# A sixth modulation block's sums moved behind two row products, its broadcasts moved one group on, four residual loads moved back, and another first PSUM bank

## The chip, the cores and the metric

The kernel runs on one core of a Trainium2 chip. Its time is the device time of one execution in microseconds (us); lower is better. A core has five engines that work beside each other and wait for each other through semaphores: TensorE (PE, matmuls), VectorE (DVE), ScalarE (ACT), GpSimd (POOL) and SyncE (SP, which here issues most of the transfers). Each engine takes its instructions in the order in which the program gives them.

## What is computed

One layer of a residual block over 1024 positions of width 1024, in float32. Six rows of 1024 (shift, scale and gate for each of two halves) come from the conditioning vector c through `w_ada`; the sixth, `gate2`, is the block that this change is about.

```python
c_act = jax.nn.silu(c)
mod = (c_act @ w_ada[l] + b_ada[l])[:, None, :]
shift1, scale1, gate1, shift2, scale2, gate2 = jnp.split(mod, 6, axis=-1)
h = rms_norm(x, norm1_w[l]) * (1.0 + scale1) + shift1
x = x + gate1 * hybrid_mixer(h, w_in[l], ...)      # projections, gated DeltaNet, short conv, @ w_out
h = rms_norm(x, norm2_w[l]) * (1.0 + scale2) + shift2
x = x + gate2 * swiglu(h, w_gate[l], w_up[l], w_down[l])
...
return rms_norm(x, norm_f_w)
```

## The kernel before

Positions are cut into eight tiles of 128; tiles 0 to 3 are the first half, 4 to 7 the second. A matmul has 512 columns; a float32 product is made of three matmuls of high and low parts, so each operand is split by a cast (high part) and a subtraction (low part).

Up to about 499 us of the span the order of work is planned by a small scheduler in Python (class `Sim`, line 296): tasks are coroutines, each operation is a request with a modelled cost, and the scheduler picks, engine by engine, the one that can start first, with priorities (`PR`, line 43) where several can. Its pick is written into the program as a fixed order on each engine. A task waits with `sim.wait(...)` for marks in the set `done`; a buffer or a PSUM bank is asked for and freed. Every operation of this part is recorded at line 440; what comes after it is written in program order and is recorded at lines 91 and 92. The profile therefore tells groups apart by the names of their tiles.

The pieces that matter here:

- `fill` (line 937) ends with the output projection of the first half: eight groups of 24 matmuls into tiles named `o`, first the right column half of tiles 0 to 3, then the left one. They take turns in three PSUM banks (0 to 2). `ev_o` adds each to the residual tile `x2[t]`, which the profile calls `x`. The weights for the left half (`us0`, in slots called `h`) are loaded from `w_out`, scaled and split by `w_unit` while the groups run.
- `load_y` brings the second half's products of the short convolution back from DRAM (`raw<-y_scr`) and splits them into `WQ`.
- `mod_rows` (line 1049) makes a row out of the scale column of the second norm: twice, DVE multiplies an identity by the column (`raw<-ident,s2c`), the result is split, two matmuls with a matrix of ones spread it to all partitions (tile `row`), and a copy stores it in `su` (called `u`).
- `gate5` and `ada_rows` (lines 1012 and 990) make `gate2`: for each column half eight weight tiles of 128 x 512 are loaded (`Tt<-in_w_ada_dram` and `raw<-in_w_ada_dram`), DVE sums them with `c_act` as scalars into `A` and `aacc`, the sum is split, two matmuls with ones spread it (tile `ada`), and DVE adds it to `gate`, which holds the bias. `gate` is used by `prep_gate` (line 1759), after 580 us.
- `norm0` stores tiles 0 to 3 of `x` to DRAM (`x_scr<-x`) and scales them for the second norm. It waits for `row` and for both halves of `gate5`.
- `coordinator` (line 1413) loads the residual tiles `x2` at its end, one SP transfer of 512 KB each, in the order of t.
- Behind the scheduler, `w_out_tile` does the output projection of tiles 4 to 7, `first_half` transposes the scaled tiles. They take PSUM banks in turn from `allb` (line 1472).

SP gives its transfers out in order, so one that waits for a buffer holds those behind it.

Of the kernel before, what the change touches and what calls it, by code (L numbers as in the profile page):

```python
# [10 lines left out]
F32R = mybir.dt.float32r  # L11
BF16 = mybir.dt.bfloat16
AF = mybir.ActivationFunctionType
ALU = mybir.AluOpType
# [3 lines left out]
P = 128  # L18
# [35 lines left out]
def kernel(  # L54
# [53 lines left out]
    def nm(s):  # L108
        n_id[0] += 1
        return f"{s}_{n_id[0]}"  # L110
# [185 lines left out]
    class Sim:  # L296
# [18 lines left out]
        def free(self, t):  # L315
            res, i = self.owner.pop(t.tensor.name)
            res.slots.append((max([a[4] for a in self.acc.get(t.tensor.name, [])] + [0.0]), i))
            res.slots.sort()
# [238 lines left out]
    def bank(res, name):  # L557
        return res.tile(psp, [P, HT], F32, name)

    def gt(tag, shape=(P, 4, P), dtype=F32):  # L560
        return GP[tag].tile(gp, list(shape), dtype, tag)

    def raw(shape=(P, HT), dtype=F32):
        return raws.tile(wst, list(shape), dtype, "raw")
# [10 lines left out]
    def esplit(src, hi, lo):  # L575
        ecopy(hi, src)
        DVE.tensor_tensor(lo, src, hi.bitcast(F32), ALU.subtract)
# [412 lines left out]
    def ada_rows(b, ch, ac=None, get=None):  # L990
        if ac is None:
            ac = wst.tile([P, HT], F32, name=nm("aacc"), tag="aacc", bufs=1)
        get = get or raw
        c0 = b * D + ch * HT
        for kk in range(KB):
            r = get()
            dma(r, wada[kk * P:(kk + 1) * P, c0:c0 + HT])
            if kk == 0:
                DVE.tensor_scalar(ac, r, c_act[:, 0:1], None, ALU.mult)
            else:  # L1000
                DVE.scalar_tensor_tensor(ac, r, c_act[:, kk:kk + 1], ac, ALU.mult, ALU.add)
            free(r)
        hl = [raw(dtype=F32R) for _ in range(2)]
        esplit(ac, hl[0], hl[1])
        ps = bank(chb, "ada")
        mm(ps, ones_r, hl[0], True, False)
        mm(ps, ones_r, hl[1], False, True)
        for t in hl:
            free(t)
        return ps  # L1010

    def gate5(ch):
        sim.wait(lambda: len(us0) == KB and len(us1) == KB and ("gdn", 1) in done)
        if 5 not in gates:
            g = gates[5] = wst.tile([P, D], F32, name=nm("gate"), tag="gate", bufs=1)
            dma(g, b_ada[0, 5 * D:6 * D].partition_broadcast(P))
        gc = gates[5][:, ch * HT:(ch + 1) * HT]
        ac = gt("A", (P, HT)) if ch else None
        ps = ada_rows(5, ch, ac, (lambda: gt("Tt", (P, HT))) if ch else None)
        done.add(("g5", ch))  # L1020
        DVE.tensor_tensor(gc, gc, ps, ALU.add)
        free(ps)
        if ch:
            free(ac)

# [387 lines left out]
    def coordinator():  # L1413
        nonlocal gp, x2p, b1p
        sim.wait(lambda: "ada0" in done)
        wa_ctx.__exit__(None, None, None)
        b1 = tc.tile_pool(name="b1", bufs=1, side="right", reuse_waits="tile")
        b1p = b1.__enter__()
        for hd in (0, 1):
            qkT[hd, 0] = qks.tile(b1p, [P, 2, HT], F32, "qkT")  # L1420
        done.add("b1")
        sim.wait(lambda: "h1" in done)
        x_ctx.__exit__(None, None, None)
        s_ctx.__exit__(None, None, None)
        pools["g"] = tc.tile_pool(name="gp", bufs=2, side="left", reuse_waits="tile")
        gp = pools["g"].__enter__()
        for i in range(4):
            xbd.append(gp.tile([P, 4, P], F32, name=f"xbd{i}", tag=f"xbd{i}", bufs=1))
        for t in xbd:
            POOL.memset(t, 0.0)  # L1430
        done.add("gp")
        sim.wait(lambda: "filled" in done and live[0] == 0 and all(("vt", 1, h) in done for h in heads) and
                 all(("sc", i, hf) in done and ("z", i, hf) in done for i in range(4) for hf in range(2)))
        b1.__exit__(None, None, None)
        pools["x2"] = tc.tile_pool(name="x2p", bufs=1, side="right", reuse_waits="tile")
        x2p = pools["x2"].__enter__()
        for t in range(NT):
            x2.append(x2p.tile([P, D], F32, name=f"x2_{t}", tag=f"x2_{t}"))
        for t in range(NT):
            sim.wait(lambda: len(us1) + len(us0) > min(5 + t, 12) and (t < 4 or ("chain", 1) in done))  # L1440
            dma(x2[t], xs[t * P:(t + 1) * P, :])
            done.add(("x2", t))

# [25 lines left out]
    mover[0], chain[0] = None, seq  # L1469
    g_ctx, x2_ctx = pools["g"], pools["x2"]  # L1470

    allb = Banks(list(range(8)))

    def gt(tag, shape=(P, 4, P), bufs=2):
        return gp.tile(list(shape), F32, name=nm(tag), tag=tag + "0", bufs=1)
# [3 lines left out]
    def pmm(o, l, r, s_, e_, more=False):  # L1479
        pe("pe", PE.matmul(o, l, r, start=s_, stop=e_, skip_group_check=more))  # L1480
# [31 lines left out]
    def keep_x2(t, chs):  # L1512
        for ch in chs:
            cs = slice(ch * HT, (ch + 1) * HT)
            ACT.dma_start(out=x2_scr[t][:, cs], in_=x2[t][:, cs])
# [41 lines left out]
        DVE.tensor_tensor(x2[t][:, cs], x2[t][:, cs], ps, ALU.add)  # L1557


    e_raw, e_u = {}, {}  # L1560

    def early_load(n):
# [13 lines left out]

    w_out_tile(4, 1)
    keep_x2(4, (1,))
    w_out_tile(4, 0)
    norm_tile(4)  # L1580
    first_half(range(4))
# [556 lines left out]
```

## Time and profile before

| | us |
|---|---|
| median of 3 runs | 1192.98 |
| lowest and highest of them | 1191.99, 1194.83 |
| the profiled execution's own time | 1194.26 |
| its span, first to last instruction | 1192.4 |
| mean granted clock of TensorE | 0.996 |

A row of the profile gives the engine, the line, the operation and `out<-in` by the names of tiles, the shape and a count; in the timeline a row starts with its start and length, and ends in brackets with the engine's idle time ahead of it and who ended that. Matmuls overlap, so their pitch is read from the length of many, not from a single one.

### The profile page before, as it was taken

Reading aid. Unit: us, or ns where it says so; the run is one execution under the profiler, and the core shown is the slowest. Engines: PE = TensorE matmul, PEld = TensorE weight load, DVE = VectorE, ACT = ScalarE, POOL = GpSimd, SP = SyncE. Lnnn points to the kernel's source line nnn. Section 1 sums busy time; section 2 is a strip of 40 time slices with the busy share of each in tenths; the row PEclk is TensorE's granted clock in tenths of the full one; section 3 lists DMA queues with packets and bytes.
Section 4 is the critical chain, followed back from the end, with each engine's and each line's share of the span. In section 5 each row is a group of like instructions: output and inputs, shape, how many; then the busy total and the mean of one; then the engine's idle time right before and its main releaser. Section 6 shows DMA issues by size and latency. Waiting matters only on the chain.

```text
span 1192.4 us, 16796 instructions
## 1 busy us (share of the span) xinstructions
PE 1173.7 (98%) x5723; PEld 984.7 (83%) x5723; DVE 928.9 (78%) x1738; ACT 529.3 (44%) x1118; POOL 57.2 (5%) x95
## 2 busy tenths in 40 slices
PE   8999999999999998999999999999999999999997
PEld 7888878988888987788888888888888888888886
DVE  6998989799977798757786767777767787688676
ACT  3488732359632544224543333333333365434343
POOL 2010000001000001100000000000000000000003
PEclk9999999999999999999999999999999999999999
DMA  9933455544425447423344564465544679869413
GB/s 289 299 81 111 133 171 161 160 115 136 111 47 130 136 133 271 174 77 98 124 157 161 191 225 157 142 205 185 198 165 140 211 275 397 311 199 346 144 42 141
DMA packets 175775, 207.08 MB, mean 174 GB/s; under 512 B 21829, under 2 KB 107978, under 8 KB 175690
## 3 DMA queue, kind: packets, MB, share of 16 engines
q1 hardware_dynamic: 170312, 202.85, 53.0%
q10 hardware_dynamic: 5378, 3.16, 0.9%
q8 instruction: 45, 0.74, 0.3%
q14 instruction: 40, 0.33, 0.1%
HBM read 150.91 MB, written 55.05 MB: 173 GB/s over the span
## 4 chain that ended last, share of the span: by engine, by line
PE 91%; DMA 3%; DVE 3%; ACT 1%; issue 1%; SPq 0%; DVEq 0%; ACTq 0%
PE acc L91 34%; PE acc L440 24%; PE dn L91 17%; PE o L91 4%; PE o L440 2%; PE A L440 1%; PE K L440 1%; DMA raw<-y_scr 1%; PE ada L440 1%; DMA x<-in_x_dram 1%; DMA raw<-in_w_ada_dram 1%; PE ab L440 1%; PE Q L440 1%; PE w L440 1%; PE u L440 1%; PE O L440 1%
## 5 line engine op out<-in xcount | busy, mean ns | idle before, releaser
L440 PE MATMUL acc<-h,u 128*128 128x512 f32 x1200 | 302.6, 398 | 0.0
L440 PEld LDWEIGHTS acc<-h,u 128*128 128x128 f32 x1200 | 219.0, 188 | 41.2
L91 PE MATMUL acc<-h,hl 128*128 128x512 f32 x600 | 140.0, 390 | 0.0
L91 PEld LDWEIGHTS acc<-h,hl 128*128 128x128 f32 x600 | 112.4, 188 | 23.2
L91 PE MATMUL acc<-h,u 128*128 128x512 f32 x456 | 106.1, 389 | 0.0
L91 PE MATMUL acc<-T,hl 128*128 128x512 f32 x432 | 101.3, 390 | 0.2 <-ACT cc L92 0.2
L91 PEld LDWEIGHTS acc<-h,u 128*128 128x128 f32 x456 | 85.6, 188 | 17.8
L91 PEld LDWEIGHTS acc<-T,hl 128*128 128x128 f32 x432 | 80.9, 188 | 17.3 <-ACT cc L92 0.6
L92 DVE TENSOR_TENSOR xo<-xo,dn 128x512 f32<-128x512 f32 x84 | 57.2, 686 | 44.0 <-PE dn L91 36.2
L91 PE MATMUL dn<-h,h 128*128 128x512 f32 x396 | 90.7, 389 | 0.0
L91 PEld LDWEIGHTS dn<-h,h 128*128 128x128 f32 x396 | 74.3, 188 | 15.4
L92 ACT COPY cc<-acc 128x512 f32<-128x512 f32 x66 | 38.5, 591 | 108.3 <-PE acc L91 108.3
L91 PE MATMUL acc<-T,u 128*128 128x512 f32 x360 | 84.0, 389 | 0.0
L91 PEld LDWEIGHTS acc<-T,u 128*128 128x128 f32 x360 | 67.6, 188 | 14.0
L440 ACT CAST u<-raw 128x512 fp32r<-128x512 f32 x64 | 39.8, 623 | 70.7 <-PE acc L440 64.1
L92 DVE TENSOR_TENSOR cc<-cc,acc 128x512 f32<-128x512 f32 x66 | 43.9, 684 | 29.8 <-PE acc L91 29.8
L440 DVE TENSOR_TENSOR u<-raw,u 128x512 fp32r<-128x512 f32 x82 | 56.2, 686 | 12.8 <-ACT u L440 12.0
L92 DVE TENSOR_TENSOR hl<-R,hl 128x512 fp32r<-128x512 f32 x60 | 39.5, 689 | 33.4 <-ACT hl L92 33.4
L440 DVE SCALAR_TENSOR_TENSOR cv<-pr,cols_b,cv 128x512 f32<-128x512 f32 x72 | 53.1, 747 | 1.2 <-ACT cv L440 0.9
L92 ACT CAST h<-rw 128x512 fp32r<-128x512 f32 x57 | 32.7, 618 | 41.0 <-PE dn L91 34.6
L92 DVE TENSOR_TENSOR u<-R,u 128x512 fp32r<-128x512 f32 x46 | 30.1, 688 | 20.5 <-ACT u L92 20.5
L92 ACT CAST hl<-R 128x512 fp32r<-128x512 f32 x60 | 35.6, 620 | 23.4 <-DVE R L92 10.7
(330 smaller groups left out, 2033.7 us busy)
## 6 DMA issues: line engine op xcount, KB each, us to landing
raw<-in_w_in_dram SPq DMA_DIRECT2D x82, 256.0 KB, 3.2
am_scr<-cc SPq DMA_DIRECT2D x77, 256.0 KB, 4.7
raw<-in_w_ada_dram SPq DMA_DIRECT2D x56, 256.0 KB, 3.3
rw<-am_scr SPq DMA_DIRECT2D x55, 256.0 KB, 5.0
rw<-bm_scr SPq DMA_DIRECT2D x53, 256.0 KB, 5.2
bm_scr<-raw SPq DMA_DIRECT2D x51, 256.0 KB, 5.6
R<-in_w_gate_dram SPq DMA_DIRECT2D x22, 512.0 KB, 4.1
R<-in_w_up_dram SPq DMA_DIRECT2D x22, 512.0 KB, 5.2
```

Source lines behind the costliest of these rows:

```text
L91: return call(*a, **k)
L92: ins = call(*a, **k)
L440: ins = call(*a, **k)
```

## The change

Four things. First, `gate5` starts on the mark `row` instead of the mark of the second half's chain, so its sums are planned after both row products. Second, its spreading matmuls and the adds into `gate` leave the scheduler: the split sums stay in four `Tt` tiles, and a new function `g5_rows` makes the matmuls in program order, behind the first group of `w_out_tile`. Third, the loads of residual tiles 4 to 7 wait for both halves of `gate5` instead of the chain. Fourth, `allb` starts at bank 5 instead of bank 0. The amount of arithmetic and of transfers is the same.

```diff
--- before.py
+++ after.py
@@ -990,6 +990,7 @@
     def ada_rows(b, ch, ac=None, get=None):
         if ac is None:
             ac = wst.tile([P, HT], F32, name=nm("aacc"), tag="aacc", bufs=1)
+        row = get is None
         get = get or raw
         c0 = b * D + ch * HT
         for kk in range(KB):
@@ -1000,8 +1001,10 @@
             else:
                 DVE.scalar_tensor_tensor(ac, r, c_act[:, kk:kk + 1], ac, ALU.mult, ALU.add)
             free(r)
-        hl = [raw(dtype=F32R) for _ in range(2)]
+        hl = [raw(dtype=F32R) if row else gt("Tt", (P, HT), F32R) for _ in range(2)]
         esplit(ac, hl[0], hl[1])
+        if not row:
+            return hl
         ps = bank(chb, "ada")
         mm(ps, ones_r, hl[0], True, False)
         mm(ps, ones_r, hl[1], False, True)
@@ -1009,17 +1012,16 @@
             free(t)
         return ps
 
+    g5 = {}
+
     def gate5(ch):
-        sim.wait(lambda: len(us0) == KB and len(us1) == KB and ("gdn", 1) in done)
+        sim.wait(lambda: len(us0) == KB and len(us1) == KB and "row" in done)
         if 5 not in gates:
             g = gates[5] = wst.tile([P, D], F32, name=nm("gate"), tag="gate", bufs=1)
             dma(g, b_ada[0, 5 * D:6 * D].partition_broadcast(P))
-        gc = gates[5][:, ch * HT:(ch + 1) * HT]
         ac = gt("A", (P, HT)) if ch else None
-        ps = ada_rows(5, ch, ac, (lambda: gt("Tt", (P, HT))) if ch else None)
+        g5[ch] = ada_rows(5, ch, ac, (lambda: gt("Tt", (P, HT))) if ch else raw)
         done.add(("g5", ch))
-        DVE.tensor_tensor(gc, gc, ps, ALU.add)
-        free(ps)
         if ch:
             free(ac)
 
@@ -1437,7 +1439,7 @@
         for t in range(NT):
             x2.append(x2p.tile([P, D], F32, name=f"x2_{t}", tag=f"x2_{t}"))
         for t in range(NT):
-            sim.wait(lambda: len(us1) + len(us0) > min(5 + t, 12) and (t < 4 or ("chain", 1) in done))
+            sim.wait(lambda: len(us1) + len(us0) > min(5 + t, 12) and (t < 4 or ("g5", 0) in done and ("g5", 1) in done))
             dma(x2[t], xs[t * P:(t + 1) * P, :])
             done.add(("x2", t))
 
@@ -1469,7 +1471,7 @@
     mover[0], chain[0] = None, seq
     g_ctx, x2_ctx = pools["g"], pools["x2"]
 
-    allb = Banks(list(range(8)))
+    allb = Banks([5, 6, 7, 3, 4, 0, 1, 2])
 
     def gt(tag, shape=(P, 4, P), bufs=2):
         return gp.tile(list(shape), F32, name=nm(tag), tag=tag + "0", bufs=1)
@@ -1557,6 +1559,14 @@
         DVE.tensor_tensor(x2[t][:, cs], x2[t][:, cs], ps, ALU.add)
 
 
+    def g5_rows():
+        for ch in range(2):
+            ps = allb.get("row")
+            pmm(ps, ones_r, g5[ch][0], True, False)
+            pmm(ps, ones_r, g5[ch][1], False, True)
+            cs = slice(ch * HT, (ch + 1) * HT)
+            DVE.tensor_tensor(gates[5][:, cs], gates[5][:, cs], ps, ALU.add)
+
     e_raw, e_u = {}, {}
 
     def early_load(n):
@@ -1576,6 +1586,7 @@
 
     w_out_tile(4, 1)
     keep_x2(4, (1,))
+    g5_rows()
     w_out_tile(4, 0)
     norm_tile(4)
     first_half(range(4))
```

Since a scheduler decides the order, three places show what moved. The first is DVE at the end of the fifth output group's inputs. Before (`raw_4978`, `raw_5024`: the two diagonals; `raw_4984`, `raw_5028`: their low parts; `h_1_921`: the last weight part of `us0`; `A`, `aacc`: the sums):

```order
L440 SCALAR_TENSOR_TENSOR raw_4828<-raw_4828,cols_a,gate_1301 128x512
L440 TENSOR_TENSOR raw_4984<-raw_4978,raw_4983 128x512
L440 TENSOR_TENSOR x_3_4748<-x_3_4748,o_4951 128x512
L440 TENSOR_TENSOR h_1_921_4994<-raw_4828,h_1_921_4994 128x512
L440 TENSOR_SCALAR A_5010<-Tt_5011,c_act 128x512
L440 TENSOR_TENSOR raw_5024<-ident,s2c 128x512
L440 TENSOR_SCALAR aacc_5013<-raw_5014,c_act 128x512
L440 SCALAR_TENSOR_TENSOR A_5010<-Tt_5021,c_act,A_5010 128x512
L440 TENSOR_TENSOR raw_5028<-raw_5024,raw_5027 128x512
```

And in the changed kernel (`raw_4974`, `raw_5010`: the diagonals):

```order
L440 SCALAR_TENSOR_TENSOR raw_4825<-raw_4825,cols_a,gate_1301 128x512
L440 TENSOR_TENSOR raw_4980<-raw_4974,raw_4979 128x512
L440 TENSOR_TENSOR x_3_4748<-x_3_4748,o_4943 128x512
L440 TENSOR_TENSOR h_1_921_4990<-raw_4825,h_1_921_4990 128x512
L440 TENSOR_TENSOR raw_5010<-ident,s2c 128x512
L440 TENSOR_TENSOR raw_5013<-raw_5010,raw_5012 128x512
L440 TENSOR_SCALAR A_5033<-Tt_5034,c_act 128x512
L440 TENSOR_SCALAR aacc_5036<-raw_5037,c_act 128x512
L440 SCALAR_TENSOR_TENSOR A_5033<-Tt_5041,c_act,A_5033 128x512
```

The second diagonal and its low part stood behind one and three steps of the sums; now all four operations of the row products are ahead of the first step.

The second place is DVE some twenty operations earlier, where the second half's y tiles are split. Before:

```order
L440 TENSOR_TENSOR Tt_4346<-y_4835,Tt_4346 128x512
L440 SCALAR_TENSOR_TENSOR so_4836<-so_4836,nq_3641 128x4
L440 TENSOR_TENSOR h_1_895_4846<-raw_4764,h_1_895_4846 128x512
L440 TENSOR_TENSOR kt_4871<-Tt_4346,at_4870 128x512
L440 TENSOR_TENSOR x_1_4746<-x_1_4746,o_4814 128x512
L440 TENSOR_TENSOR Tt_4347<-y_4860,Tt_4347 128x512
L440 TENSOR_TENSOR u_3345<-u_3345,ro_4838 128x512
```

Now:

```order
L440 TENSOR_TENSOR Tt_4346<-y_4831,Tt_4346 128x512
L440 SCALAR_TENSOR_TENSOR so_4832<-so_4832,nq_3641 128x4
L440 TENSOR_TENSOR h_1_895_4842<-raw_4764,h_1_895_4842 128x512
L440 CAST WQ_4797<-raw_4782 128x512
L440 TENSOR_TENSOR kt_4867<-Tt_4346,at_4866 128x512
L440 TENSOR_TENSOR x_1_4746<-x_1_4746,o_4811 128x512
L440 TENSOR_TENSOR Tt_4347<-y_4856,Tt_4347 128x512
L440 TENSOR_TENSOR u_3345<-u_3345,ro_4834 128x512
```

One cast, `WQ_4797<-raw_4782`, is new on DVE; it was ScalarE's before. Around it the low parts of `WQ` and the gated outputs (`Tt`, `kt`) stand in a slightly other order.

The third place is SP's queue of transfers behind the loads of tiles 0 to 3. Before:

```order
L440 DMA x_2_4747<-in_x_dram 128x1024
L440 DMA x_3_4748<-in_x_dram 128x1024
L440 DMA x_4_4749<-in_x_dram 128x1024
L440 DMA x_5_4750<-in_x_dram 128x1024
L440 DMA raw_4782<-y_scr 128x512
L440 DMA raw_4793<-y_scr 128x512
L440 DMA x_6_4751<-in_x_dram 128x1024
L440 DMA raw_4809<-in_w_out_dram 128x512
L440 DMA x_7_4752<-in_x_dram 128x1024
L440 DMA raw_4828<-in_w_out_dram 128x512
L440 DMA raw_4918<-y_scr 128x512
L440 DMA raw_4937<-y_scr 128x512
```

Now, at the same place:

```order
L440 DMA x_2_4747<-in_x_dram 128x1024
L440 DMA x_3_4748<-in_x_dram 128x1024
L440 DMA raw_4782<-y_scr 128x512
L440 DMA raw_4792<-y_scr 128x512
L440 DMA raw_4807<-in_w_out_dram 128x512
L440 DMA raw_4825<-in_w_out_dram 128x512
L440 DMA raw_4909<-y_scr 128x512
L440 DMA raw_4924<-y_scr 128x512
```

and further on, behind the sixteen loads of `w_ada`:

```order
L440 DMA Tt_5119<-in_w_ada_dram 128x512
L440 DMA raw_5124<-in_w_ada_dram 128x512
L440 DMA x_4_4749<-in_x_dram 128x1024
L440 DMA x_5_4750<-in_x_dram 128x1024
L440 DMA x_6_4751<-in_x_dram 128x1024
L440 DMA x_7_4752<-in_x_dram 128x1024
L440 DMA x_scr<-x_0_4745 128x1024
```

Tiles 4 to 7 have gone from among the y and weight loads to a place between the last load of `w_ada` and the stores of tiles 0 to 3.

## Prediction

> **What bounds the kernel now.** The page's first part comes first: TensorE (PE) is busy for nearly the whole span, so only its idle time, and time at a lower clock, can be won without removing matmuls.
>
> ```profile
> PE 1173.7 (98%) x5723; PEld 984.7 (83%) x5723; DVE 928.9 (78%) x1738; ACT 529.3 (44%) x1118; POOL 57.2 (5%) x95
> ```
>
> Then the view by windows (columns: stretch, its length, busy time and count for each engine, granted clock, DMA share, GB/s), cut at the stages and at 5 us around the place of the change:
>
> ```profile
> 200.00:444.00 244.00, 244.00 (x1416) 212.74 (x1414) 210.07 (x465) 122.73 (x300) 14.01 (x15) 1.00 0.44 123
> 444.00:500.00 56.00, 51.56 (x232) 41.79 (x231) 46.81 (x75) 23.27 (x62) 8.62 (x10) 0.97 0.67 238
> 500.00:580.00 80.00, 79.83 (x407) 66.84 (x406) 53.11 (x79) 30.75 (x59) 4.69 (x11) 1.00 0.34 112
> ...
> 455.00:460.00 5.00, 5.00 (x26) 4.10 (x25) 4.88 (x10) 3.33 (x13) 1.60 (x3) 1.00 1.03 405
> ...
> 475.00:480.00 5.00, 2.49 (x6) 2.01 (x7) 4.08 (x7) 0.62 (x1) 0.00 (x0) 0.70 0.76 270
> 480.00:485.00 5.00, 5.00 (x23) 4.11 (x22) 3.52 (x6) 0.59 (x1) 0.00 (x0) 0.96 0.87 278
> ...
> 495.00:500.00 5.00, 4.22 (x19) 3.20 (x18) 3.24 (x4) 0.93 (x2) 1.76 (x2) 1.00 0.23 92
> ```
>
> PE is never idle from 200 to 444 us and for 0.17 us from 500 to 580 us; between them, from 444 to 500 us, it loses 4.4 us and a part of its clock. This is the stretch where the output projection's last groups, the row products and the sixth modulation block meet, and all that the change touches lies in it. PE's timeline shows the two gaps (in brackets: idle before, and who ended it):
>
> ```profile
> 469.11 0.40 PE L440 MATMUL o<-h,h 128*128 128x512 f32 x1
> ...
> 470.74 3.11 PE L440 MATMUL o<-h,h 128*128 128x512 f32 x13
> 477.51 0.79 PE L440 MATMUL row<-raw,ones 128*128 128x512 f32 x1 [3.66 <-ACT raw L440]
> ...
> 492.25 6.06 PE L440 MATMUL o<-h,h 128*128 128x512 f32 x26
> 499.10 0.50 PE L91 MATMUL o<-L,WQ 128*128 128x512 f32 x1 [0.78 <-DVE x L440]
> 499.43 0.39 PE L91 MATMUL o<-wu,WQ 128*128 128x512 f32 x1
> ```
>
> The chain of work that ended last (start, length, what) says why the first one arises:
>
> ```profile
> 469.94 5.70 DMA Tt<-in_w_ada_dram
> ...
> 475.66 0.49 DVE A L440
> 476.15 0.61 DVE raw L440
> ...
> 476.84 0.63 ACT raw L440
> ...
> 477.51 0.79 PE row L440
> 478.30 1.71 PE o L440 x4
> 480.01 0.43 PE row L440
> 480.44 10.25 PE o L440 x45
> ```
>
> VectorE (DVE) takes its queue in order. The first step of the sums (`A<-Tt`) stood there for its load, and behind it the diagonal (`raw<-ident,s2c`) of the second row product. ScalarE's cast, and with it PE's `row` matmul in the middle of the fifth output group, waited for that.
>
> **The change part by part.** One matmul at full clock takes 10.25 / 45 = 0.2278 us (last row).
>
> *Sums behind the row products.* The DVE order of the changed kernel has both row products ahead of the first sum. Gap: 470.74 + 13 x 0.2278 = 473.70 to 477.51, so 3.81 us. Behind it PE ran slowly: six matmuls from 477.51 to 480.44 took 2.93 us, against 6 x 0.2278 = 1.37; 1.56 us lost. Together 5.37 us, if the second row product isn't late for another reason. The trace shows the granted clock at 0.70 there, and the four matmuls at 478.30 at 0.43 us each. [...]
>
> What is late next? The fifth group starts at 469.11 if nothing before it moves. Its second row product stands after 18 matmuls (469.11 + 4.10 = 473.21) with the high part and after 21 (473.89) with the low part. DVE sets when they are ready:
>
> ```profile
> 454.18 0.43 DVE L440 CAST h<-raw 128x512 fp32r<-128x512 f32 x1
> 455.04 0.69 DVE L440 TENSOR_TENSOR u<-u,ro 128x512 f32<-128x512 f32 x1 [0.44 <-POOL ro L440]
> ...
> 456.32 0.68 DVE L440 TENSOR_TENSOR h<-raw,h 128x512 fp32r<-128x512 f32 x1
> ...
> 461.23 0.69 DVE L440 TENSOR_TENSOR u<-u,ro 128x512 f32<-128x512 f32 x1 [0.29 <-POOL ro L440]
> ...
> 470.64 0.68 DVE L440 TENSOR_TENSOR h<-raw,h 128x512 fp32r<-128x512 f32 x1
> 475.66 0.49 DVE L440 TENSOR_SCALAR A<-Tt,c_act 128x512 f32<-128x512 f32 x1 [4.34 <-DMA Tt<-in_w_ada_dram]
> ```
>
> From 456.32 to 471.32 it has hardly a gap. The changed order brings the same operations up to that last `h<-raw,h`, and one cast more (0.43), which ScalarE did before: 471.75. The diagonal adds 0.61, ScalarE's cast 0.63 with some 0.1 of hand-over, DVE's low part 0.68: 472.36, 473.1, 473.8. PE wants them at 473.21 and 473.89: on time, by a tenth. If the two POOL waits (0.44 and 0.29) close up it is on time by 0.8; if a load holds DVE up, PE waits. I put 0.4 us for a new wait here, between none and the 1.8 of the first rival, nearer to none since every row but the load speaks for it.
>
> *Banks from elsewhere.* The first group written in program order took bank 0, still to be read by DVE after the last scheduled group; now it takes bank 5. The gap 492.25 + 26 x 0.2278 = 498.17 to 499.10 is 0.93, and the first matmul took 0.33 in place of 0.23: 1.03 us. Banks 6, 7 and 3 follow, which the chain stage's transposes and the row products used last.
>
> *Broadcasts among the second half's groups.* Four matmuls and two DVE adds leave the seventh group and come after the first program-order group: 4 x 0.23 us on PE in both kernels, no gain. The adds go to where DVE waits for PE; these rows cover them:
>
> ```profile
> 501.81 1.28 DVE L440 SCALAR_TENSOR_TENSOR x<-x,st,u 128x1024 f32<-128x1024 f32 x1 [2.77 <-DMA x_scr<-x]
> 504.94 0.69 DVE L92 TENSOR_TENSOR x<-x,o 128x512 f32<-128x512 f32 x1 [1.85 <-PE o L91]
> 510.49 0.69 DVE L92 TENSOR_TENSOR x<-x,o 128x512 f32<-128x512 f32 x1 [4.86 <-PE o L91]
> ```
>
> Without that cover they would cost 1.2 us. The new wait, PE on the split sums, is met: ScalarE's view has the second sum's cast, the last but one step of the splits, at
>
> ```profile
> 490.47 0.62 ACT L440 CAST raw<-aacc 128x512 fp32r<-128x512 f32 x1
> ```
>
> and PE comes to them one group after the last scheduled one: 498.17 - 6.4 + 24 x 0.2278 = 497.2.
>
> *Later residual loads.* Tiles 4 to 7 move on SP's queue from among the y and weight loads to behind the 16 weight loads of the sums. SP's timeline (start, length, count):
>
> ```profile
> 450.83 0.94 SPq L440 DMA_DIRECT2D raw<-y_scr  x2
> ...
> 483.40 0.44 SPq L440 DMA_DIRECT2D raw<-in_w_ada_dram  x1
> 484.05 15.34 SPq L440 DMA_DIRECT2D x_scr<-x  x4
> ```
>
> The issues of 440 to 510 us by group (count, size, median us to landing):
>
> ```profile
> x<-in_x_dram SPq DMA_DIRECT2D x8, 512.0 KB, 6.8
> ...
> raw<-in_w_ada_dram SPq DMA_DIRECT2D x8, 256.0 KB, 5.7
> x_scr<-x SPq DMA_DIRECT2D x4, 512.0 KB, 2.6
> ...
> raw<-y_scr SPq DMA_DIRECT2D x4, 256.0 KB, 8.6
> ```
>
> The y loads lose 2.1 MB ahead of them, 5.2 us at 405 GB/s, so they land earlier, not later; nothing on PE waited for them alone, so I count nothing. Tile 4 is wanted when its first group ends, at 497.2. Issued near 484 behind a weight load that lands at 483.4 + 5.7 = 489.1, all four are in by 489.1 + 5.2 = 494.3. Nothing waits.
>
> **Sum.** 5.37 + 1.03 - 0.4 = 6.0 us. Against the profiled execution (1194.26 us, span 1192.4) this gives 1188.3; that execution lies 1.3 us above the median of the runs shown (1192.98), from which the same gain gives **1187.0**. Everything behind 500 us hangs on PE (0.17 us idle up to 580) and shifts with it.
>
> **The rivals.** *First: the gap shrinks but stays.* The DVE cast that is new needs the first y load. Issued a little ahead of the old 450.83, say 450.3, and landing after the old median of 8.6, it comes at 458.9; DVE would reach it at 457.0. Then all of DVE is 1.9 late and PE waits 475.7 - 473.9 = 1.8: gain 6.4 - 1.8 = 4.6, 1188.4. Against it: the 2.1 MB ahead are gone, and without those the load lands near 456. *Second: PE gains nothing.* What PE needs behind the row product, the last weight part (`h<-raw,h`), was done at 471.32 and can't hold it until 477.5. But the first transposes want x tiles 0 to 3 scaled. Before, the last scaling ended at 501.81 + 1.28 = 503.09, while PE came to the transposes 11.4 us after 499.10, at 510.5. Now PE comes at 504.1: if the scaling stayed where it was the margin would be 1.0 us. A scaling 6 us later than before would give all back: 1193. *Third, slower than before.* The scaling of tile 3 also waits until its store has read the tile, and the stores of tiles 0 to 3 now stand behind the four loads. With the loads done at 494.3, four stores of 0.52 MB at 405 GB/s end at 499.5, and about 1 us of landing and 1.28 of scaling give 501.8; margin 2.3 us. For each us beyond it PE waits one, and a wait over 3.7 us would bring the slow clock (1.56) again; so from a delay of 2.3 + 4.9 = 7.2 us on it is slower than before: at 10 us late PE waits 7.7, pays 1.56 more and has won 6.4: 1195.8. For it speaks this row, where loads issued one behind another took up to 10 us to land, against 2.6 for a store alone:
>
> ```profile
> DMA to landing us min/median/max: 6.0/6.8/10.0
> ```
>
> [...] Against the rival: it needs three times the margin that these rows leave.
>
> **How the numbers follow.** Forecast 0.75, about 1187 (1185.0 to 1188.6: a median of few runs moved from 1191.99 to 1194.83); first rival 0.12 (1188 to 1190.5); second 0.07 (1191 to 1194); third 0.06 (1193 to 1197). The range 1185.0 to 1190.6 takes in the forecast and the first rival, and the bounds of the new wait. A measurement of this kernel tells 0.2% (2.4 us) from no change: faster by more than that 0.87 (forecast and first rival), within it 0.08 (the second, and a little of the third), slower 0.05.
>
> **What would show it.** In the changed kernel's windows: 470 to 485 us with PE busy throughout and the clock at 1.00; a `row` matmul with an idle time under 1 us; no idle time ahead of the first L91 matmul; the first L91 transposes some 6 us earlier and without a wait; DVE's first `A<-Tt` still waiting for its load, now with nobody behind it. The prediction is wrong if PE waits over 2 us at `row`, if the transposes wait for `x`, or if a gap appears behind 500 us that wasn't there.

## The result, and the profile after

| | us |
|---|---|
| before, median of 6 runs beside the changed kernel (lowest, highest) | 1193.53 (1191.99, 1195.70) |
| changed, median of 6 runs (lowest, highest) | 1187.32 (1186.06, 1189.51) |
| ratio, 95% interval | 0.9949 (0.9934 to 0.9964) |
| the profiled execution of the changed kernel: its time, its span | 1186.41, 1184.6 |
| mean granted clock of TensorE | 0.998 |

The medians differ by 6.2 us; 6.0 were forecast, and 1187.0 for the time. First, the page's first line of the changed kernel:

```profile
PE 1171.7 (99%) x5723; PEld 984.3 (83%) x5723; DVE 928.4 (78%) x1739; ACT 528.4 (45%) x1117; POOL 55.6 (5%) x95
```

The work is the same, and PE's share has risen from 98 to 99%. The view by windows (columns as before: stretch, length, busy time of PE, PEld, DVE, ACT and POOL, clock, DMA share, GB/s):

```profile
444.00:500.00 56.00, 56.00 (x259) 46.05 (x258) 47.07 (x76) 22.20 (x61) 9.38 (x12) 1.00 0.68 248
...
475.00:480.00 5.00, 5.00 (x24) 4.14 (x23) 5.00 (x8) 0.00 (x0) 0.00 (x0) 1.00 1.04 386
480.00:485.00 5.00, 5.00 (x24) 4.14 (x23) 4.32 (x8) 0.14 (x1) 0.00 (x0) 1.00 1.04 397
485.00:490.00 5.00, 5.00 (x24) 4.14 (x23) 2.48 (x4) 4.24 (x8) 1.56 (x5) 1.00 1.02 410
```

PE is busy for all 56 us from 444 to 500, where it was busy for 51.56, and the clock, 0.70 and 0.96 between 475 and 485 us before, is 1.00. The chain of waits of the changed kernel (start, length, what) is PE alone through the place of the change:

```profile
443.12 2.52 PE o L440 x11
...
471.95 0.23 PE row L440
472.18 0.47 PE o L440 x2
472.65 0.23 PE row L440
472.88 17.69 PE o L440 x78
490.57 5.59 PE o L91 x24
496.17 0.94 PE row L91 x4
497.11 5.55 PE o L91 x24
502.65 1.75 PE tr L91 x16
```

The second row product comes in its place without a wait, and the first L91 group follows the last scheduled one at once. The four `row` matmuls of L91 are the moved broadcasts. The same two marks in the chain of the kernel before:

```profile
444.63 2.53 PE o L440 x11
...
510.45 1.75 PE tr L91 x16
```

From the first `o` group to the first transposes of L91 PE needs 502.65 - 443.12 = **59.53 us**, and 510.45 - 444.63 = **65.82** before: 6.29 us less. This **stretch** is the measure for the experiments: it has all that the change moves, and leaves out where the execution stood by then (442.7 to 446.0 us in the profiles below, with the same code ahead of it). The spans differ by 7.8 us; the 1.5 beyond the 6.29 were there at 443 us already.

DVE's timeline of the changed kernel (start, length, what; in brackets the idle time ahead and who ended it):

```profile
456.05 0.43 DVE L440 CAST WQ<-raw 128x512 fp32r<-128x512 f32 x1 [0.58 <-DMA raw<-y_scr]
...
469.81 0.68 DVE L440 TENSOR_TENSOR raw<-ident,s2c 128x512 f32<-128x512 f32 x1
471.24 0.69 DVE L440 TENSOR_TENSOR raw<-raw,raw 128x512 fp32r<-128x512 f32 x1 [0.74 <-ACT raw L440]
472.76 0.49 DVE L440 TENSOR_SCALAR A<-Tt,c_act 128x512 f32<-128x512 f32 x1 [0.83 <-DMA Tt<-in_w_ada_dram]
...
491.23 1.28 DVE L440 SCALAR_TENSOR_TENSOR x<-x,st,u 128x1024 f32<-128x1024 f32 x1 [3.75 <-DMA x_scr<-x]
492.44 0.68 DVE L440 TENSOR_TENSOR x<-x,o 128x512 f32<-128x512 f32 x1
...
496.27 1.28 DVE L440 SCALAR_TENSOR_TENSOR x<-x,st,u 128x1024 f32<-128x1024 f32 x1 [0.77 <-POOL st L440]
```

The first sum (`A<-Tt`) still waits for its load, now behind the diagonal and the split, and only other sums are behind it. The split is done at 471.24 + 0.69 = 471.93, and PE wants it at 472.65: a margin of 0.7 us. The last scaling is done at 497.55, and the transposes begin at 502.65: a margin of 5.1. The 3.75 us behind a store at 491.23 stand ahead of the first of the four scalings; in the kernel before only the last one waited for a store (2.77). The addition behind that wait (`x<-x,o` at 492.44) is the one that empties the last scheduled group's bank. PE began on another bank at 490.57 and didn't need it.

The four moved matmuls stood behind 19 of the seventh group's 24 matmuls and now stand behind the first L91 group. That is 5 + 24 + 24 = 53 matmuls later, so two groups on rather than the one that the title says.

### The profile page after: what moved, and what is told of

It is laid out like the page before. It is cut to its first block, busy times and chain, and to the rows that moved or that the text cites. A ratio compares the mean times of both kernels' runs of the same rounds, so it can differ in the third digit from the quotient of the medians.

```text
span 1184.6 us, 16797 instructions
## 1 busy us (share of the span) xinstructions
PE 1171.7 (99%) x5723; PEld 984.3 (83%) x5723; DVE 928.4 (78%) x1739; ACT 528.4 (45%) x1117; POOL 55.6 (5%) x95
## 4 chain that ended last, share of the span: by engine, by line
PE 95%; DVE 2%; DMA 1%; ACT 1%; issue 0%; SPq 0%; DVEq 0%; ACTq 0%
PE acc L91 34%; PE acc L440 26%; PE dn L91 17%; PE o L91 4%; PE o L440 4%; PE A L440 1%; PE K L440 1%; PE ab L440 1%; PE Q L440 1%; PE u L440 1%; PE w L440 1%; PE P L440 1%; PE kk L440 1%; PE qk L440 1%; DMA wr<-in_w_in_dram 1%; PE O L440 1%
## 5 line engine op out<-in xcount | busy, mean ns | idle before, releaser
L91 PE MATMUL acc<-h,hl 128*128 128x512 f32 x600 | 140.1, 390 | 0.0
L91 PEld LDWEIGHTS acc<-h,hl 128*128 128x128 f32 x600 | 112.4, 188 | 23.2
L91 PE MATMUL acc<-h,u 128*128 128x512 f32 x456 | 106.1, 389 | 0.0
L91 PE MATMUL acc<-T,hl 128*128 128x512 f32 x432 | 101.3, 390 | 0.2 <-ACT cc L92 0.2
L91 PEld LDWEIGHTS acc<-h,u 128*128 128x128 f32 x456 | 85.6, 188 | 17.7
L91 PEld LDWEIGHTS acc<-T,hl 128*128 128x128 f32 x432 | 80.9, 188 | 17.2 <-ACT cc L92 0.6
L91 PE MATMUL dn<-h,h 128*128 128x512 f32 x396 | 90.7, 389 | 0.0
L91 PEld LDWEIGHTS dn<-h,h 128*128 128x128 f32 x396 | 74.3, 188 | 15.4
L91 PE MATMUL acc<-T,u 128*128 128x512 f32 x360 | 84.0, 389 | 0.0
L91 PEld LDWEIGHTS acc<-T,u 128*128 128x128 f32 x360 | 67.6, 188 | 14.0
```

The costliest lines, as they stand in the source:

```text
L91: return call(*a, **k)
```

## The experiments

All are readings of one profiled execution for the stretch, the idle time of PE in it and who ended that, beside the medians of the runs. "Rest" is the stretch less 59.53 (the stretch of the changed kernel, without idle time or slow clock), less the idle time, and in the sixth row less the 3.64 us of its 16 added matmuls: what the slow clock and the first matmuls behind a wait cost (the one at 499.10 in the kernel before took 0.33 us in place of 0.23). Each stretch is that of one execution. Where there are several runs, the gain by the stretch and the gain by the ratio lie within 0.8 us of each other; only the kernel before with the new banks is further off (0.8 us slower by the stretch, 0.8 faster by the ratio).

| kernel | median us (runs) | ratio, interval | stretch us | idle of PE, us | rest |
|---|---|---|---|---|---|
| changed | 1187.32 (6) | 0.9949 (0.9934 to 0.9964) | 59.53 | none | 0 |
| before | 1193.53 (6) | 1 | 65.82 | row 3.66, L91 0.78 | 1.85 |
| changed, old banks | 1191.42 (10) | 0.9982 (0.9971 to 0.9992) | 64.43 | L91 3.21 | 1.69 |
| before, new banks | 1192.40 (10) | 0.9993 (0.9982 to 1.0003) | 66.63 | row 2.54, ada 2.03 | 2.53 |
| before, sums behind the row products | 1189.26 (8) | 0.9964 (0.9954 to 0.9974) | 62.12 | ada 0.60, L91 1.50 | 0.49 |
| before, 16 matmuls ahead of the second row product | 1193.73 (1) | | 66.00 | ada 1.49, L91 0.78 | 0.56 |
| changed, early residual loads | 1186.70 (5) | 0.9949 (0.9931 to 0.9967) | 59.87 | first row product 0.12 | 0.22 |
| changed, broadcasts planned by the scheduler | 1186.74 (4) | 0.9947 (0.9930 to 0.9964) | 59.55 | none | 0.02 |
| changed, early residual loads and old banks | 1190.02 (7) | 0.9969 (0.9958 to 0.9980) | 61.92 | L91 2.25 | 0.14 |
| before, sums moved and new banks | 1187.50 (4) | 0.9956 (0.9939 to 0.9972) | 60.23 | ada 0.46 | 0.24 |
| changed, 4 more diagonals | 1188.85 (1) | | 61.48 | row 1.69 | 0.26 |
| changed, 6 more diagonals | 1192.41 (1) | | 65.62 | row 3.12 | 2.97 |
| changed, 10 more diagonals | 1196.86 (1) | | 68.61 | row 6.02 | 3.06 |

The ratios are to runs of before on the same chip, whose medians lay between 1192.99 and 1194.23.

### The sums alone

```diff
-        sim.wait(lambda: len(us0) == KB and len(us1) == KB and ("gdn", 1) in done)
+        sim.wait(lambda: len(us0) == KB and len(us1) == KB and "row" in done)
```

> The kernel before with the sums of the sixth block started on the mark of the row products and nothing else changed (broadcasts planned by the scheduler, early residual loads, bank 0). Theory of the prediction: the gap at `row` and the slow clock behind it (5.37 us) go, the bank's wait of 1.0 stays: stretch 60.4 us. Rival: PE then comes to bank 0 while DVE is still busy with sums and scalings, and waits longer for it than before: 61 to 62.5. Rival that the order is not the cause: 65 to 66.

PE's timeline of this kernel, all the waits of the stretch:

```profile
485.98 0.50 PE L440 MATMUL ada<-raw,ones 128*128 128x512 f32 x1 [0.60 <-ACT raw L440]
...
494.15 0.50 PE L91 MATMUL o<-L,WQ 128*128 128x512 f32 x1 [1.50 <-DVE x L440]
```

The wait at `row` is gone, and the stretch is 3.70 us shorter, not 5. Two things took the difference: the broadcasts (`ada`), at which PE now comes earlier than the sums end (though the scheduler has put them five matmuls further on, right ahead of the eighth group), and bank 0, whose wait has grown from 0.78 to 1.50 since PE comes to it earlier too.

### The slow clock filled

16 matmuls into the row product's bank, right ahead of the first matmul of the second row product, which starts that bank anew:

```diff
+    def warm_matmul(o, l, r, **k):
+        for _ in range(16):
+            seq("pe", nc.tensor.matmul(o, l, Y[0][4][0], start=True, stop=True))
+        return nc.tensor.matmul(o, l, r, **k)
...
-            mm(ps, ones_r, hl[0], True, False)
+            if ch:
+                mover[0].op("pe", "matmul", warm_matmul, (ps, ones_r, hl[0]), dict(start=True, stop=False))
+            else:
+                mm(ps, ones_r, hl[0], True, False)
```

> The kernel before with 16 extra matmuls of 512 columns (3.64 us at 0.2278) directly ahead of the second row product's first matmul; their result is overwritten by it. They fill the 3.81 us in which PE was idle. Theory: the slow clock behind the gap comes from PE's idleness, so the six matmuls behind it take 1.37 in place of 2.93 us: stretch 65.82 - 1.56 = 64.3 us (up to 64.5 for what of the gap isn't filled). Rival: the slow matmuls have another cause (operands, DVE or DMA traffic): stretch 65.8, and the matmuls behind the gap still at 0.43 us each.

PE's timeline:

```profile
472.60 3.89 PE L1051 MATMUL row<-h,ones 128*128 128x512 f32 x16
476.34 0.39 PE L1052 MATMUL row<-raw,ones 128*128 128x512 f32 x1
476.57 1.09 PE L440 MATMUL o<-h,h 128*128 128x512 f32 x4
...
489.59 0.50 PE L440 MATMUL ada<-raw,ones 128*128 128x512 f32 x1 [1.49 <-ACT raw L440]
```

The added matmuls fill the wait, and the four `o` behind it take 1.09 us, their tail included, where the chain of before has 1.71: the slow clock is gone (1.00 from 475 to 485 us, 0.70 and 0.96 before). The stretch is 66.00, as long as before. PE came to the broadcasts some 1.4 us earlier and waited 1.49 there: it began them 489.59 - 443.38 = 46.2 us behind the first `o` group, by the same timeline 490.53 - 444.47 = 46.1 in the kernel before. So in the kernel before, the slow clock's loss was no price of its own: the end of the sums, which DVE had only begun behind the load, set when PE could go on, and the slow clock lay in time that PE would else have waited two groups later. This rests on one execution of this kernel.

### The banks

The new list alone, and the changed kernel with the old one:

```diff
-    allb = Banks(list(range(8)))
+    allb = Banks([5, 6, 7, 3, 4, 0, 1, 2])
```

> The kernel before with the first program-order group in bank 5 and nothing else changed. Theory of the prediction: the 0.78 us wait (1.03 us by pitch) ahead of the first L91 matmul goes, the gap at `row` stays: stretch 64.8 us against 65.82. If the group waited for something else there, no change: 65.8.

Put on the kernel before, the list removes the wait at L91, but this execution has a new one at the broadcasts (PE's timeline):

```profile
474.63 0.50 PE L440 MATMUL row<-raw,ones 128*128 128x512 f32 x1 [2.54 <-ACT raw L440]
...
488.94 0.50 PE L440 MATMUL ada<-raw,ones 128*128 128x512 f32 x1 [2.03 <-ACT raw L440]
```

The interval of the ratio, 0.9982 to 1.0003, can't tell a gain of up to 2 us from none. The 1.0 us of the prediction is neither shown nor excluded by it; the stretch of the one profile went against it, by the same end of the sums: 488.94 - 442.72 = 46.2 us behind the first `o` group once more, though PE had waited 1.1 us less at `row`. With it came slow clock behind the 2.03, by an estimate from its 3.4 us half of that, 1.7 us (last section).

> The changed kernel with the first program-order group back in bank 0; nothing else differs. Read from the stretch between the start of the first `o` group and the start of the first transposes on PE: 65.82 us before (444.63 to 510.45), 59.53 in the changed kernel (443.12 to 502.65). Theory of the prediction: the wait for bank 0 costs the 1.0 us that it cost before, stretch 60.5. Second theory: the wait is as long as DVE needs to read tile 3's group, and in the changed kernel DVE does that only at 492.44 to 493.12, behind a wait for a store, while PE is done at about 490.4: a wait of 2.6 to 2.8 us, stretch 62.2, clock still full. Third theory: the bank is worth nothing, 59.5.

Taken from the changed kernel, the list is worth far more than 1.0: 64.43 - 59.53 = 4.90 us of the stretch, and 1191.42 - 1187.32 = 4.1 by the medians. All of it is at L91: 3.21 of waiting, and 1.69 mostly of slow clock behind it (0.66 from 495 to 500 us). PE's row, then DVE's:

```profile
495.18 0.50 PE L91 MATMUL o<-L,WQ 128*128 128x512 f32 x1 [3.21 <-DVE x L440]
```

```profile
493.24 1.28 DVE L440 SCALAR_TENSOR_TENSOR x<-x,st,u 128x1024 f32<-128x1024 f32 x1 [4.50 <-DMA x_scr<-x]
494.44 0.68 DVE L440 TENSOR_TENSOR x<-x,o 128x512 f32<-128x512 f32 x1
```

The addition that empties bank 0 stands behind a scaling, and that waits 4.50 us for a store of `x`. The changed kernel has the same wait (3.75, above) and shows nothing of it, since PE no longer needs that bank.

Are the late residual loads what holds the store up? The changed kernel with the old condition for these loads and the old banks, beside the one with the old condition alone:

```diff
-            sim.wait(lambda: len(us1) + len(us0) > min(5 + t, 12) and (t < 4 or ("g5", 0) in done and ("g5", 1) in done))
+            sim.wait(lambda: len(us1) + len(us0) > min(5 + t, 12) and (t < 4 or ("chain", 1) in done))
```

> The changed kernel with the early residual loads and the old order of banks. Measured is the stretch from the first group of the output projection's last part to the first L91 transposes: 59.53 us in the changed kernel, 59.87 with early loads alone, 64.43 with the old banks alone. Theory: with the old banks PE waited 3.21 us (and ran slowly for 1.7 more) because the late loads push the x_scr stores back, DVE's scaling waits for its store (4.50) and the addition that empties bank 0 stands behind that scaling. With early loads the scaling doesn't wait, and the wait at the first L91 matmul is 0 to 1.5 us: stretch 59.9 to 61.4, no slow clock. Rival: the wait for bank 0 has nothing to do with the loads: 64.4 again.

DVE's timeline of it:

```profile
490.43 1.29 DVE L440 SCALAR_TENSOR_TENSOR x<-x,st,u 128x1024 f32<-128x1024 f32 x1 [0.73 <-POOL st L440]
492.77 1.28 DVE L440 SCALAR_TENSOR_TENSOR x<-x,st,u 128x1024 f32<-128x1024 f32 x1 [1.06 <-POOL st L440]
493.98 0.68 DVE L440 TENSOR_TENSOR x<-x,o 128x512 f32<-128x512 f32 x1
```

With early loads the scalings ahead of that addition wait for GpSimd, 0.73 and 1.06 us, and for no store. The old banks then cost 61.92 - 59.87 = 2.05 us, against 4.90 with the late loads. Of the 2.85 between them, 1.1 is waiting and 1.8 lies in the rest: the clock is 0.66 from 495 to 500 us with the late loads, and 1.00 from 465 to 505 with the early ones. By the ratios the two costs are 2.4 and 3.9 us, and the intervals of the two kernels with old banks overlap (0.9958 to 0.9980, 0.9971 to 0.9992), so the wait for the store is shown by the rows, and the size of its price less surely. The theory holds in kind; its size was off, since the wait left at L91 was 2.25 us and not 0 to 1.5: two scalings and two waits for GpSimd still stand ahead of the addition.

### Residual loads and broadcasts

The old condition for the loads alone (the diff just above):

> The changed kernel with the loads of residual tiles 4 to 7 where they were (among the y loads). Theory of the prediction: they cost nothing in either place, stretch 59.5 to 59.8 us. Rival: with 2.1 MB ahead of them the y loads land later, ScalarE and DVE are held up and the second row product comes late, PE waits 1 to 2 us at `row`: 60.5 to 61.5.

And the broadcasts and their adds back under the scheduler, with all else as changed. It puts the first of them behind one matmul of the eighth group:

```diff
...
-        g5[ch] = ada_rows(5, ch, ac, (lambda: gt("Tt", (P, HT))) if ch else raw)
+        gc = gates[5][:, ch * HT:(ch + 1) * HT]
+        ps = ada_rows(5, ch, ac, (lambda: gt("Tt", (P, HT))) if ch else None)
         done.add(("g5", ch))
+        DVE.tensor_tensor(gc, gc, ps, ALU.add)
+        free(ps)
...
-    g5_rows()
```

> The changed kernel with the four broadcast matmuls of the sixth block and the two adds into gate planned by the scheduler again (it puts them near the start of the eighth group); sums behind the row products, late residual loads and bank 5 stay. Theory of the prediction: four matmuls cost the same wherever they stand, stretch 59.5 us. Rival: the eighth group starts at about 485 and meets them after one matmul, but the low parts of the two sums are ready only at 486.2 and 486.9 in the changed kernel: a wait of 0.5 to 1.2 us, stretch 60.0 to 60.7.

Each alone changes nothing that the runs can tell: stretches of 59.87 and 59.55, ratios of 0.9949 and 0.9947. With both taken away, which is the kernel before with the sums moved and the new banks:

> Before, with the sums behind the row products and the new order of banks, but the broadcasts in the seventh group and early residual loads. With the sums alone moved PE still waited 0.60 us at the first broadcast and 1.50 at the first L91 matmul (stretch 62.12). Theory: the banks take away the second wait and nothing comes in its place: 60.1 to 60.4, so two of the change's four parts bring nearly all of it, and each of the other two only covers that 0.60. Rival: something else is late behind the bank (the scaling of tile 3 ahead of the transposes, which ended at 498.13 where the transposes began at 505.5), 61 or more; or, as with the banks alone, PE arrives earlier at the broadcasts and waits there: 61 to 62 with the wait at ada over 1.5.

PE's only wait in that stretch:

```profile
485.72 0.50 PE L440 MATMUL ada<-raw,ones 128*128 128x512 f32 x1 [0.46 <-ACT raw L440]
```

The stretch is 60.23, so two of the four parts bring 5.6 of the 6.3 us. The other two each cover what is left, by two ways: the moved broadcasts come two groups later, and with the late loads the sums begin earlier. The first sum began 473.00 - 443.71 = 29.3 us behind the first `o` group with late loads and the broadcasts at the eighth group, and 473.64 - 443.32 = 30.3 here (by DVE's timelines). Busy DMA engines aren't the main cause: from 465 to 470 us both profiles show 39 GB/s (DMA share 0.18 and 0.14). SP issued the first of these loads 24.8 us behind the first `o` group with late loads and 25.4 here; the load then took 0.4 us less with late loads, and DVE waited 0.92 us for it there and 1.47 here. The medians, 1187.50 and 1187.32, can't tell the two kernels apart.

### How much of a wait PE can have at the row product

More diagonals into the same tile, ahead of the second row product's own (4, then 6 and 10):

```diff
+    def again(*a):
+        for _ in range(4):
+            seq("dve", nc.vector.tensor_tensor(*a))
+        return nc.vector.tensor_tensor(*a)
...
-            DVE.tensor_tensor(dg, bc1(ident, 4), bc2(s2c[:, 4 * ch:4 * ch + 4], P), ALU.mult)
+            mover[0].op("dve", "tensor_tensor", again if ch else nc.vector.tensor_tensor,
+                        (dg, bc1(ident, 4), bc2(s2c[:, 4 * ch:4 * ch + 4], P), ALU.mult), {})
```

> The changed kernel with the second diagonal made five times in place of once (four more DVE operations of about 0.6 us, 2.4 to 2.9 in all) ahead of the second row product. In the changed kernel its high part was cast by 471.20 and wanted at 471.95, its low part done by 471.93 and wanted at 472.65: margin 0.7 us. Theory: PE waits 1.7 to 2.2 us at `row` and pays no slow clock since the gap is short: stretch 61.2 to 61.8. Rival: any gap at that place brings the slow clock: 62.8 to 63.4. Rival: the row products don't hold PE at all: 59.5.

> The changed kernel with six extra diagonals ahead of the second row product. Four made PE wait 1.69 us at row, at full clock behind it (stretch 61.48); ten made it wait 6.02, with 3.1 us lost to the slow clock behind it (68.61). Six should give a wait of 1.69 + 2 x 0.61 = 2.9. Theory: a wait short of some 3.2 us costs itself alone: stretch 62.5 to 62.8, clock 1.00 behind it. Rival: the clock falls already behind waits of 2 to 3 us (with the banks alone a wait of 2.03 had a clock of 0.66 behind it): 64.0 to 64.5.

> The same with ten more diagonals (6.0 to 7.2 us). Theory: PE waits 5.3 to 6.5 us at `row`, and now the slow clock comes on top (1.56): stretch 66.4 to 67.6 us, no better than before the change. Without the slow clock 64.8 to 66.0.

Four cost 1.95 us. By DVE's timelines four more take 2.89 us, six 4.34 and ten 7.25, so 0.72 each and not the 0.61 that was expected. The rows with four and with six:

```profile
469.76 2.86 DVE L1053 TENSOR_TENSOR raw<-ident,s2c 128x512 f32<-128x512 f32 x4
472.65 0.69 DVE L1054 TENSOR_TENSOR raw<-ident,s2c 128x512 f32<-128x512 f32 x1
```

```profile
469.18 4.31 DVE L1053 TENSOR_TENSOR raw<-ident,s2c 128x512 f32<-128x512 f32 x6
473.52 0.69 DVE L1054 TENSOR_TENSOR raw<-ident,s2c 128x512 f32<-128x512 f32 x1
```

PE waited 1.69, 3.12 and 6.02 us, each time 1.2 less than what was added. So the margin is real, but it is 1.2 us here, where the changed kernel's own profile shows 0.7. The difference is DVE's 0.58 us behind the y load, which these three profiles don't have: DVE came to the second diagonal 26.1 us behind the first `o` group, and 469.81 - 443.12 = 26.7 us behind it in the changed kernel's. With four, the wait costs itself and 0.26, at a clock of 1.00. Six made PE wait 3.12 and cost 2.97 more; ten 6.02 and 3.06 more. The theory for six, that a wait short of some 3.2 us costs itself alone, has fallen. PE's clock in stretches of 2 us, with six more:

```profile
474.00:476.00 2.00, 1.03 (x3) 0.84 (x4) 1.26 (x4) 0.62 (x1) 0.00 (x0) 0.52 0.13 49
476.00:478.00 2.00, 2.00 (x6) 1.61 (x5) 1.09 (x3) 0.59 (x1) 0.00 (x0) 0.50 0.59 180
478.00:480.00 2.00, 2.00 (x6) 1.52 (x6) 0.36 (x1) 0.00 (x0) 0.00 (x0) 0.50 0.99 321
480.00:482.00 2.00, 2.00 (x9) 1.59 (x8) 2.00 (x4) 0.00 (x0) 0.00 (x0) 0.77 0.93 311
```

and in the kernel before:

```profile
476.00:478.00 2.00, 0.49 (x1) 0.49 (x2) 2.00 (x5) 0.62 (x1) 0.00 (x0) 0.75 0.56 213
478.00:480.00 2.00, 2.00 (x6) 1.52 (x6) 1.75 (x3) 0.00 (x0) 0.00 (x0) 0.50 0.83 266
480.00:482.00 2.00, 2.00 (x10) 1.62 (x9) 1.02 (x2) 0.59 (x1) 0.00 (x0) 0.90 0.74 215
```

In stretches of 0.2 us the profile of before has a clock of 1.00 up to 476.8 us, 0.50 from 477.0 to 480.2 and 1.00 from 480.4 on, with 0.96 and 0.51 in the two between. If the other profiles too have only 0.5 and 1, a stretch of 2 us at a mean of c holds 4 x (1 - c) us of the slow one. That is an estimate: 1.92 + 2 + 2 + 0.92 = 6.8 us with six more diagonals, and 1.0 + 2.0 + 0.4 = 3.4 before, as the finer stretches have it. The longer wait of before (3.66) had the shorter slow time.

### More loads ahead of the stores

Tiles 4 to 7 loaded twice more, 8 transfers of 512 KB with the same data, ahead of the stores of tiles 0 to 3:

```diff
+        for t in (4, 5, 6, 7) * 2:
+            dma(x2[t], xs[t * P:(t + 1) * P, :])
```

> The changed kernel with tiles 4 to 7 loaded three times in place of once: eight more transfers of 512 KB (4.2 MB, 10.5 us at 400 GB/s) on SP's queue between the first loads of these tiles and the stores of tiles 0 to 3. It tests the third rival of the prediction. In the changed kernel tile 3's scaling ended at 497.55 and the transposes began at 502.65: margin 5.1 us. Theory of that rival: the stores move by 10.5 us, PE waits 5.4 us ahead of the transposes and pays 1.5 us of slow clock: stretch about 66.5. If half of the transfers go beside other work, or the stores are served between the loads, the wait is shorter: 59.5 to 62.

One run: 1194.87 us, beside 1194.23 of before. The summary of SP's waits (who was waited for: us in total, times, longest), and PE's timeline at the transposes:

```profile
SPq L440 <- DMA x<-in_x_dram: 11.6, 8, 5.1
```

```profile
505.70 0.33 PE L91 MATMUL tr<-ident,x 128*128 128x128 f32 x1 [0.27 <-DVE x L440]
506.92 0.33 PE L91 MATMUL tr<-ident,x 128*128 128x128 f32 x1 [0.89 <-DVE x L440]
508.15 0.33 PE L91 MATMUL tr<-ident,x 128*128 128x128 f32 x1 [0.90 <-DVE x L440]
509.40 2.82 PE L91 MATMUL tr<-ident,x 128*128 128x128 f32 x12 [0.92 <-DVE x L440]
```

SP waited for each tile's earlier load before the next into it, and issued the stores from 498.22 us on, 52.3 behind the first `o` group; in the changed kernel that was 481.12 and 38.0, so 14 us earlier. DVE's scalings came all four behind that, from 504.36, and PE waited for each. The transposes began on time by the stretch (59.90), but ended 66.48 us behind the first `o` group, where the changed kernel's end 61.28 behind it: 5.2 us lost, 7 expected. The third rival's mechanism is real, and it took some 14 us of delay to the stores to bring it out. The run doesn't part the two causes of that delay. SP held each load back until the earlier one into the same tile had landed. The DMA engines were meanwhile nearly always busy (DMA share 1.05, 1.04, 0.88 and 1.03 in the stretches of 5 us from 480 to 500), and at 400 GB/s (388, 409, 304 and 403 in these) the eight loads alone, 4.2 MB, are an estimated 10.5 us.

## Why the prediction was right

The time (1187.32 against 1187.0), the sign and the cause (DVE's queue ahead of the second row product) came out as forecast. The sum is right in the whole; its terms are not right one by one.

*Sums behind the row products: 5.37, less 0.4 for a new wait.* The gap and the slow clock are gone from that place, and the new wait is none: DVE's split came 0.7 us ahead of PE, in the forecast margin of 0.1 to 0.8. But alone this part brings 3.70 us of the stretch, not 5. The step that failed is "what is late next?": it was asked of the row product and of what follows the last group, and not of the sums' own end. They end some 3.3 us earlier than before (PE's first broadcast 485.98 - 443.22 = 42.8 us behind the first `o` group, 46.1 before, by PE's timelines). PE has won more than that by then, so that it stands at the broadcasts (0.60), and it comes to bank 0 earlier (1.50 in place of 0.78). That the slow clock's 1.56 was counted as won in full has the same fault: filled with other matmuls it brought nothing.

*Banks from elsewhere: 1.03.* That is what bank 0 cost in the profile of before, not what it would cost in the changed kernel. Behind the moved sums the list is worth 62.12 - 60.23 = 1.89, and with the late loads beside it 4.90. The mis-sized term is this one, and its excess makes up for what the first lacks: 3.70 + 1.89 + 0.70 for the other two = 6.29.

*Broadcasts and residual loads: nothing.* Not quite: one of the two is needed for the last 0.70 us of the stretch, and either will do (0.36 and 0.68 apart). The late loads' price, 64.43 - 61.92 = 2.5 us (1.55 of it in the rest, so slow clock), is paid only with the old banks; "nothing waits" was true for PE in the changed kernel, and not for DVE, which waits 3.75 us for a store at its first scaling; with early loads it waits for one only at the last scaling (1.56).

*The rivals.* First: DVE did wait for the first y load, 0.58 us, and hadn't made it up by the row product: six other profiles of changed kernels with late loads have no such wait, and DVE is 0.6 us earlier there. It used up margin, and PE didn't wait. Second: the scaling was done 5.1 us ahead of the transposes. Third: 2.3 us of margin were forecast and 5.1 measured. The forecast had all stores behind all loads, with a last scaling that ends at 501.8 by the clock of the profile before; it ended at 497.55, which is 499.1 by that clock. The forecast's 1 us for a store's landing was the author's estimate; the four stores took 2.6 us from issue to landing in both kernels (median), of which 0.52 MB at 405 GB/s are 1.3. The row that the rival leaned on (6.0, 6.8, 10.0) is of all eight tile loads and shows how long they took, not what a store behind them does. The changed kernel's profile is nearer to it: the first store was issued at 481.12, and DVE waited for a store until 491.23, with the DMA engines busy all the while (share 1.04 and 1.02 from 480 to 490). And the 3.7 us from which the forecast counted the slow clock, the one wait of before (3.66), are no such border: 2.03 brought it (last section).

*The median.* Prediction and measurement differ by 0.3 us, less than the medians of before scatter between chips (1192.98 to 1193.55).

## What to carry to other kernels

A wait in a profile says what can be won at that place and not what the end of the kernel wins: ask for every engine behind it what it does when the waiter comes some microseconds earlier, and first of all for the work that was moved back to make room. Edits that look free or worth a fixed amount may cover one another: the same bank list was worth about 2 us of the stretch with early loads and 4.9 with late ones (1.7 of these slow clock), and each of two others was worth nothing while its partner stood. So measure parts by leaving one out and by putting one in; neither alone tells what a part is for.

## What the runs showed of the hardware

These are readings of one execution each. By the reckoning above the time of the slow clock was 3.4 us behind waits of 3.66 (before), 3.21 (changed, old banks: clocks of 0.90, 0.50 and 0.74 from 494 to 500) and 2.03 (before, new banks, at `ada`: 0.60 and 0.54 from 490 to 494). It was 6.8 behind waits of 3.12 and 6.02 (6 more diagonals, and 10: 0.64, 0.50, 0.50 and 0.65 from 478 to 486). There was none (clock 1.00 in the stretches behind the wait) behind 1.49 (16 matmuls ahead), 1.50 (the sums alone), 1.69 (4 more diagonals), 2.25 (early residual loads and old banks) and 2.54 (before, new banks, at `row`). The view by windows with the new banks alone, behind the 2.03:

```profile
490.00:492.00 2.00, 2.00 (x7) 1.59 (x6) 1.63 (x4) 1.60 (x4) 1.02 (x4) 0.60 0.00 0
492.00:494.00 2.00, 2.00 (x6) 1.53 (x6) 2.00 (x3) 1.15 (x2) 0.63 (x2) 0.54 0.25 98
```

So in these runs a longer wait didn't always cost more, nor is there one length from which on it cost: 2.03 brought the slow clock and 2.54 didn't. Why, no run shows.

Nor did the slow time begin with the wait. In the kernel before it began at 477.0, 0.5 us ahead of the matmul that ended the wait (477.51). By the same reckoning it began at 495.6 with the old banks, 0.4 behind that matmul (495.18), and at 490.4 with the new banks alone, 1.5 behind it (488.94). With six more diagonals PE worked in it from 474.97 to 480.92; half of that, (480.92 - 474.97) / 2 = 2.97 us, is the rest in the table.
